# Where the constant tiles of a two-layer decoder trunk start in on-chip memory

## The chip, the core and the metric

The kernel runs on one core of one Trainium2 chip. The core has a matmul engine (TensorE, PE in the profile, with its weight loads listed apart as PEld), VectorE (DVE), ScalarE (ACT), GpSimd (POOL) and SyncE (SP), which here only issues transfers. Operands of a matmul come from the on-chip memory SBUF, 128 partitions wide; a tile takes the same range of bytes in each partition, so "a tile starts at byte 18720" means that byte of each partition. Products go to PSUM. The metric is the device time of one execution in microseconds (us); less is better.

## The reference

Two layers act on x of 512 positions by 1024 channels, in float32:

```python
for l in range(DEPTH):                      # 2
    h = rmsnorm(x, norm_mix_g[l])
    proj = einsum('bsd,de->bse', h, w_in[l])
    # split into: attention q, k, v (4 heads, two maps of 64 each), retention q, k, v, gate
    # (4 heads), short convolution b, c, x (256 each), gates of three branches (3 x 1024)
    o_da  = diff_attention(...)             # softmax map 0 minus lambda times map 1, times v
    o_ret = retention(...) * silu(r_g)
    o_sc  = sc_b * causal_dwconv(sc_c * sc_x, ...)
    y = sum over branches of sigmoid(gate + b_gate) * (o_branch @ w_branch)
    x = x + y @ w_out[l]
    h = rmsnorm(x, norm_ffn_g[l])
    g, u = split(h @ w_ffn_in[l])           # 2816 each
    x = x + (silu(causal_dwconv(g)) * u) @ w_ffn_out[l]
return x
```

## The kernel before, in words

x is held transposed, as eight tiles `x0` to `x7` of 128 channels by 512 positions (2048 bytes per partition). Every float32 product is made from operands in two parts, a rounded part (hi) and the rest (lo), by three matmuls: hi x hi, hi x lo and lo x hi (`mm3`, lines 145 to 149). Weights come as float32 tiles over SP's queue, and `split_w` (lines 130 to 140) makes their two parts with one ScalarE copy and one VectorE subtraction. The parts of x, times the gain of the norm, are made by `split_x` (lines 239 to 243) four times in the program, before the mixers and before the FFN of each layer, into tiles `xh{k}` and `xl{k}`; a pool of one buffer per name gives each new pair the place of the old one. The norm's factor itself is applied to the products.

A matmul holds a stationary operand of 128 x 128 and streams a moving operand past it. Two arrangements matter here:

- The transposed projections (`proj_T`: three parts of the short convolution for each of two halves and 24 gates, 30 tiles in a layer, product names ptsc and ptg) and the FFN's first matrix (22 tiles of g and 22 of u in a layer, pg and pu) use the weights as stationary operand and the parts of x, 512 columns, as moving one: 8 blocks of channels x 3 = 24 matmuls for each tile.
- The projections by position (`natural`, lines 301 to 330: pnrqk and pnrvg with 512 columns, pnh of each head with 384) use the parts of x as stationary operand and move the weights: 4 blocks of positions x 8 x 3 = 96 matmuls.

The other large products have no operand from x: the branches (pb, moving om, the mixers' outputs), the output projection (po0 to po7, moving y) and the FFN's second matrix (p2, moving act), all 512 columns wide.

In a layer come first pnrqk and pnrvg; then a woven stretch, in which the steps of the retention and of the heads' attention (many small VectorE and ScalarE operations between small matmuls) alternate with heads' projections, short convolution, gates and branches as filler; then gates and branch of the attention, the output projection, and the FFN in three groups of 8, 7 and 7 tiles, each with its share of the second matrix. The order on each engine is planned when the program is built, from this order in the text, by a scheduler with a model of times; waits between engines are put in by the same planner from the tiles that instructions read and write.

Tiles lie in pools, one after the other, each rounded up to a multiple of 32 bytes. In the program of before the pool of constants (`cp`) begins at byte 16512, and its tiles follow in the order in which the text first asks for them:

| Tiles | First byte | Past a multiple of 512 |
|---|---|---|
| ident, ones | 16512, 17024 | 128 |
| warm, par0, par1 | 17536, 17568, 18144 | 128, 160, 224 |
| x0 to x7 | 18720 to 33056 | 288 |
| rope_t, gtab_t | 35104, 37152 | 288 |
| mask_t, bias_t | 37280, 37792 | 416 |
| pad0, pad1 | 45984, 48064 | 416, 448 |
| state, qz0, qz1 | 50144, 53216, 57312 | 480 |
| xh0, xl0 to xh7, xl7 | 61408 to 92128 | 480 |
| rb | 94176 | 480 |

The weights' pool follows at 94208, the work tiles' pool (which holds om, y and act) at 135168 and the small tiles' pool at 219136, each a multiple of 512; the slots of the first two have sizes that are multiples of 2048 bytes.

The text that asks for the constants stands at lines 165 to 227, and for the parts of x in `split_x`:

Of the kernel before, what the change touches and what calls it, by code (L numbers as in the profile page):

```python
# [11 lines left out]
F32 = mybir.dt.float32  # L12
F32R = mybir.dt.float32r
# [24 lines left out]
SINGLE = 1  # L38
SOME = 5
# [4 lines left out]
# columns of the packed per-layer parameters  # L44
# [5 lines left out]
def trunk(ctx, tc, xT, wr, wh, wt, wda, wret, wsc, wo, wf, w2, par, lamp, relb, onehot, mask, rope, gtab, out):  # L50
# [30 lines left out]
    def weave(first, second):  # L81
        """Steps of first, each followed by about COVER us of second."""
        due = 0.0
        for _ in first:
            due += COVER
            while due > 0.0:
                cost = next(second, None)
                if cost is None:
                    break
                due -= cost  # L90
        run(second)

    def staggered(tasks):
        """Tasks side by side, a step of each at a time, each from its own start on."""
        t = 0
        while tasks:
            live = []
            for start, task in tasks:
                if start <= t and next(task, DONE) is DONE:
                    continue  # L100
                live.append((start, task))
            tasks = live
            t += 1
            yield
# [12 lines left out]
    def ordered(i):  # L117
        """The program's first loads follow one another as they are written."""
        if starting[0]:
            tc.keep_in_program_order(i)  # L120
        return i
# [23 lines left out]
    def mm3(o, a, b, start, stop):  # L145
        """o += a.T @ b in float32, from operands in two exact parts."""
        T.matmul(o, a[0], b[0], start=start, stop=False)  # L147
        T.matmul(o, a[0], b[1], start=False, stop=False)  # L148
        T.matmul(o, a[1], b[0], start=False, stop=stop)  # L149

    def split(src, hi, lo, g=None):
        """float32 src (times a column) as two float32r parts."""
        if g is None:
            A.copy(hi, src)
            V.tensor_tensor(lo, src, hi.bitcast(F32), ALU.subtract)
        else:
            A.activation(hi, src, AF.Copy, scale=g)
            V.scalar_tensor_tensor(lo, src, g, hi.bitcast(F32), ALU.mult, ALU.subtract)
        return hi, lo
# [6 lines left out]
    ident = cp.tile([P, P], F32, name="ident")  # L166
    make_identity(nc, ident)
    ones = cp.tile([P, P], F32, name="ones")
    G.memset(ones, 1.0)
    warm = cp.tile([P, 1], F32, name="warm")  # L170
    A.activation(warm, ones[:, 0:1], AF.Tanh)
    # the array's clock rises with use: bring it up while the first loads are under way
# [7 lines left out]
    x = [cp.tile([P, S], F32, name=f"x{k}") for k in range(KT)]  # L180
# [5 lines left out]
    rope_t = cp.tile([P, 2, ST, 64], F32, name="rope_t")  # L186
    gtab_t = cp.tile([P, ST, 8], F32, name="gtab_t")
    mask_t = cp.tile([P, P], F32, name="mask_t")
    bias_t = cp.tile([P, H, S], F32, name="bias_t")
# [8 lines left out]
    def biases():  # L198
        """The negated relative bias, with the causal mask, as a Toeplitz tile per head."""
        rb = cp.tile([BUCKETS + 1, H], F32, name="rb")  # L200
        V.memset(rb[BUCKETS : BUCKETS + 1], -BIG)
        G.dma_start(rb[:BUCKETS], relb)
        line = dr.tile([H, 640], F32, name="line")
        for a, b in ((0, 512), (512, 640)):
            oh = temp(f"oh{a}", b - a)[: BUCKETS + 1]
            G.dma_start(oh, onehot[:, a:b])
            ps = aux(f"psb{a}")
            T.matmul(ps[:H, : b - a], rb, oh, start=True, stop=True)
            row = temp(f"line{a}", b - a)[:H]
            V.tensor_copy(row, ps[:H, : b - a])  # L210
            G.dma_start(line[:, a:b], row)
        skew = dr.tile([H, P * 640], F32, name="skew")
        G.dma_start(skew.rearrange("h (p n) -> h p n", n=640), line.unsqueeze(1).broadcast_to([H, P, 640]))
        src = skew[:, 127 : 127 + 639 * P].rearrange("h (p n) -> p h n", n=639)
        G.dma_start(bias_t, src[:, :, :S])

    # zero columns in front of what the convolutions read
# [4 lines left out]
    # the retention's states and queries of two heads, on the diagonal blocks  # L222
    state = cp.tile([P, 2, ST - 1, P], F32R, name="state")
    G.memset(state.bitcast(F32), 0.0)
    qz = [cp.tile([P, ST, 2, P], F32R, name=f"qz{a}") for a in range(2)]
# [3 lines left out]
    def rsqrt(f, v, n, name):  # L229
        """v ** -0.5: a first guess from the exponent, and Newton's steps to float32's last bit."""  # L230
        t = sp.tile([P, n], F32, tag=f"nt{n}", name=f"nt{name}", bufs=2)
        V.tensor_scalar(t.bitcast(I32), v.bitcast(I32), 1, None, ALU.logical_shift_right)
        V.tensor_scalar(f.bitcast(I32), t.bitcast(I32), -1.0, float(0x5F3759DF), ALU.mult, ALU.add)
        for _ in range(3):
            V.scalar_tensor_tensor(t, f, -0.5, f, ALU.mult, ALU.mult)
            V.tensor_tensor(t, t, v, ALU.mult)
            V.scalar_tensor_tensor(f, t, 1.5, f, ALU.add, ALU.mult)

    def split_x(l, which, name, k):
        """x times its gain in two parts."""  # L240
        hi = cp.tile([P, S], F32R, tag=f"xh{k}", name=f"xh{k}_{name}")
        lo = cp.tile([P, S], F32R, tag=f"xl{k}", name=f"xl{k}_{name}")
        return split(x[k], hi, lo, pars[l][:, which + k : which + k + 1])

    def norm_x(name):
        """1 / rms of x by column and by row."""
# [18 lines left out]
    def project(xg, ps, w):  # L265
        """ps[e, s] = sum over d of w[d, e] x[d, s], for 128 columns of a weight."""
        for k, xk in enumerate(xg):
            sl = slice(k * P, (k + 1) * P)
            mm3(ps, (w[0][:, sl], w[1][:, sl]), xk, k == 0, k == len(xg) - 1)

    def rms_cols(sq, n, scale, name):
        """(mean square + eps) ** -0.5 over the last axis of sq [p, n, d]."""
        ms = small(n, f"ms{name}")
        V.tensor_reduce(ms, sq, AX.X, ALU.add)
        V.tensor_scalar(ms, ms, scale, EPS, ALU.mult, ALU.add)
        f = small(n, f"f{name}")
        rsqrt(f, ms, n, name)
        return f

    def transposes(src, name):  # L280
        """Four 128 x 128 blocks of src(st), side by side in a bank."""
        ps = aux(name)
        for st in range(ST):
            T.transpose(ps[:, st * P : (st + 1) * P], src(st), ident)
        return ps
# [6 lines left out]
    def layer(l):  # L292
# [8 lines left out]
        def natural(src, w, name, evacuate):  # L301
            """w columns of the input projection by position, one bank per 128 positions; in steps."""
# [70 lines left out]
        # -lambda, in every partition  # L373
# [23 lines left out]
        def head_chunk(h):  # L397
            """Head h of the attention: queries and keys by position, values in two parts."""
# [26 lines left out]
        def attention(h):  # L425
            """A head in steps: scores and softmax of a block of queries, the difference of its two
            maps, its transpose, its product with the values; neighbouring blocks overlap."""
# [3 lines left out]
            # a map's queries in two parts above each other, against keys whose first part stands twice  # L431
# [22 lines left out]
            def scores(i):  # L454
# [8 lines left out]
                for m in range(2):  # L463
                    # a map in either half of the array's rows
# [9 lines left out]
            def combine(i):  # L474
                # e0 / z0 - lambda e1 / z1, times z0
# [15 lines left out]
            def values(i):  # L491
                # against both parts of v at once, side by side
# [41 lines left out]
        kn = (wide(f"knh{L}"), wide(f"knl{L}"))  # L534

        def retention(p):
# [34 lines left out]
            def scores(b):  # L571
                # two blocks of positions, both heads
# [97 lines left out]
        def side(b, src, mats):  # L670
            """The gated sum over the short convolution (b = 2) and the retention (b = 1)."""
# [12 lines left out]
        # the retention and the heads, with what does not depend on them between their steps  # L684
# [73 lines left out]
def _consts():  # L758
    """Tables that depend on the shapes alone."""
# [18 lines left out]
    # the retention's decay between positions i and j, g ** i for queries, g ** -j / 8 for keys  # L778
# [11 lines left out]
def _layout(i):  # L790
    """The inputs as the program's tensors: tiles of weights that are contiguous by partition."""
    C = np.ascontiguousarray

    def cols(w, n):
        # [L, K*P, n*P] -> [L, n, P, K*P]
# [6 lines left out]
    def rows(w, n, width):  # L802
        # two rows of tiles beside each other
        return C(w.reshape(DEPTH, 4, 2, P, n, width).transpose(0, 4, 1, 3, 2, 5)).reshape(DEPTH, n, 4, P, 2 * width)

    def two(w):
        # two tiles of columns beside each other
# [53 lines left out]
```

## Time and profile before

| What | Value |
|---|---|
| Median of 3 runs | 1589.82 us (1586.66 to 1590.9) |
| Span of the profiled execution | 1584.9 us |
| TensorE matmuls, busy | 7286, 1577.1 us (100%) |
| VectorE busy | 980.8 us (62%) |
| ScalarE busy | 627.1 us (40%) |
| GpSimd busy | 9.1 us (1%) |
| Moved by transfers | 147.04 MB, mean 93 GB/s |
| Mean granted TensorE clock | 1.000 |

The span runs from the first to the last instruction of the profiled execution; no other time of that execution is listed, and the runs' times include what lies around it. A line of the profile names the source line (L148), the engine, the operation, the tile written and the tiles read (`out<-in`, buffer numbers and the layer's number left out), shapes, how many (x64), and times. In a table by stretches of time, each engine has its busy time and, in brackets, how many instructions ran. Matmuls are pipelined: their printed durations overlap, and a new one starts before the last has ended.

### The profile page before, as it was taken

Reading aid. Unit: us, or ns where it says so; the run is one execution under the profiler, and the core shown is the slowest. Engines: PE = TensorE matmul, PEld = TensorE weight load, DVE = VectorE, ACT = ScalarE, POOL = GpSimd, SP = SyncE. Lnnn points to the kernel's source line nnn. Section 1 sums busy time; section 2 is a strip of 40 time slices with the busy share of each in tenths; the row PEclk is TensorE's granted clock in tenths of the full one; section 3 lists DMA queues with packets and bytes.
Section 4 is the critical chain, followed back from the end, with each engine's and each line's share of the span. In section 5 each row is a group of like instructions: output and inputs, shape, how many; then the busy total and the mean of one; then the engine's idle time right before and its main releaser. Section 6 shows DMA issues by size and latency. Waiting matters only on the chain.

```text
span 1584.9 us, 18971 instructions
## 1 busy us (share of the span) xinstructions
PE 1577.1 (100%) x7286; PEld 1303.8 (82%) x7286; DVE 980.8 (62%) x1826; ACT 627.1 (40%) x1057; POOL 9.1 (1%) x21
## 2 busy tenths in 40 slices
PE   9999999999999999999999999999999999999998
PEld 7898887888888888888889988888888888888887
DVE  7488777554566456456656887765555763564562
ACT  4455664233333233233425565642333431332331
POOL 1000000000000000000000000000000000000000
PEclk9999999999999999999999999999999999999999
DMA  5322232232333332333322222322323333323323
GB/s 184 123 91 73 61 100 74 92 100 74 106 94 93 93 93 90 97 106 88 98 80 91 72 85 69 94 74 87 98 82 93 93 93 104 94 88 100 94 87 100
DMA packets 46891, 147.04 MB, mean 93 GB/s; under 512 B 6120, under 2 KB 6519, under 8 KB 46801
## 3 DMA queue, kind: packets, MB, share of 16 engines
q1 hardware_dynamic: 45216, 143.11, 30.2%
q0 software_dynamic: 1584, 2.72, 0.5%
q8 instruction: 57, 0.93, 0.3%
q14 instruction: 34, 0.27, 0.1%
HBM read 143.70 MB, written 3.42 MB: 93 GB/s over the span
## 4 chain that ended last, share of the span: by engine, by line
PE 98%; DMA 1%; DVE 0%; ACT 0%; issue 0%; SPq 0%; ACTq 0%; DVEq 0%
PE pnrvgL L147 1%; PE pnrvgL L149 1%; PE pnrvgL L148 1%; PE pnrqkL L148 1%; PE pnrqkL L149 1%; PE pnrqkL L147 1%; PE pnh3L L148 1%; PE pnh2L L149 1%; PE pnh3L L147 1%; PE pnh1L L147 1%; PE pnh2L L147 1%; PE pnh1L L148 1%; PE pnh1L L149 1%; PE pnh3L L149 1%; PE pnh2L L148 1%; PE pnh0L L147 1%
## 5 line engine op out<-in xcount | busy, mean ns | idle before, releaser
L138 ACT CAST hi_tL<-raw_tL 128x1024 fp32r<-128x1024 f32 x60 | 63.0, 1050 | 126.1 <-DMA raw_tL<-in_wt 21.8
L138 ACT CAST hi_fuL<-raw_fuL 128x1024 fp32r<-128x1024 f32 x44 | 46.3, 1052 | 156.1 <-issue 18.0
L138 ACT CAST hi_w2L<-raw_w2L 128x896 fp32r<-128x896 f32 (+1 forms) x48 | 47.1, 982 | 142.9 <-PE p200L L148 11.9
L139 DVE TENSOR_TENSOR lo_tL<-raw_tL,hi_tL 128x1024 fp32r<-128x1024 f32 x60 | 73.4, 1223 | 17.4 <-ACT hi_tL L138 17.0
L138 ACT CAST hi_fgL<-raw_fgL 128x1024 fp32r<-128x1024 f32 x44 | 46.3, 1053 | 83.8 <-issue 13.0
L139 DVE TENSOR_TENSOR lo_fuL<-raw_fuL,hi_fuL 128x1024 fp32r<-128x1024 f32 x44 | 53.9, 1225 | 27.4 <-ACT hi_fuL L138 27.4
L139 DVE TENSOR_TENSOR lo_w2L<-raw_w2L,hi_w2L 128x896 fp32r<-128x896 f32 (+1 forms) x48 | 54.4, 1133 | 3.9 <-ACT hi_w2L L138 2.3
L139 DVE TENSOR_TENSOR lo_fgL<-raw_fgL,hi_fgL 128x1024 fp32r<-128x1024 f32 x44 | 53.6, 1219 | 3.5 <-ACT hi_fgL L138 3.5
L138 ACT CAST hi_oL<-raw_oL 128x1024 fp32r<-128x1024 f32 x16 | 16.9, 1053 | 57.2 <-PE ptg7L L148 13.4
L148 PE MATMUL pnrqkL<-lo_nrqkL,xh_mL 128*128 128x512 f32 x64 | 25.6, 400 | 0.1
L149 PE MATMUL pnrvgL<-hi_nrvgL,xl_mL 128*128 128x512 f32 x64 | 25.4, 397 | 0.0
L148 PE MATMUL pnrvgL<-lo_nrvgL,xh_mL 128*128 128x512 f32 x64 | 25.4, 396 | 0.0
L149 PE MATMUL pnrqkL<-hi_nrqkL,xl_mL 128*128 128x512 f32 x64 | 25.1, 395 | 0.0
L147 PE MATMUL pnrqkL<-hi_nrqkL,xh_mL 128*128 128x512 f32 x64 | 23.7, 405 | 1.0 <-ACT hi_nrqkL L138 1.0
L147 PE MATMUL pnrvgL<-hi_nrvgL,xh_mL 128*128 128x512 f32 x64 | 24.1, 399 | 0.0
L149 PE MATMUL pnh2L<-hi_nh2L,xl_mL 128*128 128x384 f32 x64 | 22.3, 349 | 0.0
L148 PE MATMUL pnh3L<-lo_nh3L,xh_mL 128*128 128x384 f32 x64 | 22.2, 347 | 0.0
L147 PE MATMUL pnh3L<-hi_nh3L,xh_mL 128*128 128x384 f32 x64 | 22.2, 347 | 0.0
L139 DVE TENSOR_TENSOR lo_oL<-raw_oL,hi_oL 128x1024 fp32r<-128x1024 f32 x16 | 19.6, 1225 | 4.1 <-ACT hi_oL L138 4.1
L147 PE MATMUL pnh1L<-hi_nh1L,xh_mL 128*128 128x384 f32 x64 | 21.8, 341 | 0.0
L147 PE MATMUL pnh2L<-hi_nh2L,xh_mL 128*128 128x384 f32 x64 | 21.8, 340 | 0.0
L148 PE MATMUL pnh1L<-lo_nh1L,xh_mL 128*128 128x384 f32 x64 | 21.8, 340 | 0.0
(3622 smaller groups left out, 5046.7 us busy)
## 6 DMA issues: line engine op xcount, KB each, us to landing
raw_tL<-in_wt SPq DMA_DIRECT2D x60, 512.0 KB, 3.6
raw_fgL<-in_wf SPq DMA_DIRECT2D x44, 512.0 KB, 3.5
raw_fuL<-in_wf SPq DMA_DIRECT2D x44, 512.0 KB, 3.6
raw_w2L<-in_w SPq DMA_DIRECT2D x32, 448.0 KB, 3.3
raw_oL<-in_wo SPq DMA_DIRECT2D x16, 512.0 KB, 3.6
raw_w2L<-in_w SPq DMA_DIRECT2D x16, 512.0 KB, 3.5
raw_nrvgL<-in_wr SPq DMA_DIRECT2D x8, 512.0 KB, 3.6
raw_bdL<-in_wda SPq DMA_DIRECT2D x16, 256.0 KB, 2.6
```

The costliest lines, as they stand in the source:

```text
L138: A.copy(hi, raw)
L139: V.tensor_tensor(lo, raw, hi.bitcast(F32), ALU.subtract)
L147: T.matmul(o, a[0], b[0], start=start, stop=False)
L148: T.matmul(o, a[0], b[1], start=False, stop=False)
L149: T.matmul(o, a[1], b[0], start=False, stop=stop)
```

## The change

The large constant tiles are asked for at the head of the program, before any instruction, in a new order: `ident`, `ones`, a tile `fill` of 96 floats that nothing reads or writes, the eight tiles of x, eight tiles `xs` that each hold both parts of one block of x (before two tiles, `xh` and `xl`), `state`, `qz`, `rope_t`, `mask_t` and `bias_t`. After them come warm, the parameters, gtab_t, the pads and rb, in that order. `warm` has 32 columns, of which one is used as before, and `rb` 16, of which four are used. `split_x` writes into the lasting tile `xs[k]` in place of new tiles of one name. The instructions that compute, and their shapes, are the same. Comments are taken out.

```diff
+FILL = 96
...
     ident = cp.tile([P, P], F32, name="ident")
+    ones = cp.tile([P, P], F32, name="ones")
+    cp.tile([P, FILL], F32, name="fill")
+    x = [cp.tile([P, S], F32, name=f"x{k}") for k in range(KT)]
+    xs = [cp.tile([P, 2, S], F32R, name=f"xs{k}") for k in range(KT)]
+    state = cp.tile([P, 2, ST - 1, P], F32R, name="state")
+    qz = [cp.tile([P, ST, 2, P], F32R, name=f"qz{a}") for a in range(2)]
+    rope_t = cp.tile([P, 2, ST, 64], F32, name="rope_t")
+    mask_t = cp.tile([P, P], F32, name="mask_t")
+    bias_t = cp.tile([P, H, S], F32, name="bias_t")
     make_identity(nc, ident)
-    ones = cp.tile([P, P], F32, name="ones")
     G.memset(ones, 1.0)
-    warm = cp.tile([P, 1], F32, name="warm")
-    A.activation(warm, ones[:, 0:1], AF.Tanh)
+    warm = cp.tile([P, 32], F32, name="warm")
+    A.activation(warm[:, 0:1], ones[:, 0:1], AF.Tanh)
...
-    x = [cp.tile([P, S], F32, name=f"x{k}") for k in range(KT)]
...
-    rope_t = cp.tile([P, 2, ST, 64], F32, name="rope_t")
     gtab_t = cp.tile([P, ST, 8], F32, name="gtab_t")
-    mask_t = cp.tile([P, P], F32, name="mask_t")
-    bias_t = cp.tile([P, H, S], F32, name="bias_t")
...
-        rb = cp.tile([BUCKETS + 1, H], F32, name="rb")
+        rb = cp.tile([BUCKETS + 1, 16], F32, name="rb")[:, :H]
...
-    state = cp.tile([P, 2, ST - 1, P], F32R, name="state")
     G.memset(state.bitcast(F32), 0.0)
-    qz = [cp.tile([P, ST, 2, P], F32R, name=f"qz{a}") for a in range(2)]
...
     def split_x(l, which, name, k):
-        hi = cp.tile([P, S], F32R, tag=f"xh{k}", name=f"xh{k}_{name}")
-        lo = cp.tile([P, S], F32R, tag=f"xl{k}", name=f"xl{k}_{name}")
-        return split(x[k], hi, lo, pars[l][:, which + k : which + k + 1])
+        return split2(x[k], xs[k], pars[l][:, which + k : which + k + 1])
...
     def split2(src, t, g=None):
         n = src.shape[-1]
         return split(src, t[:, 0, :n], t[:, 1, :n], g)
```

## The prediction

> **What bounds the kernel now.** I read the head of the profile page first, then TensorE's waits, then the rate of matmuls in stretches that hold one kind of matmul alone.
>
> ```profile
> span 1584.9 us, 18971 instructions
> PE 1577.1 (100%) x7286; PEld 1303.8 (82%) x7286; DVE 980.8 (62%) x1826; ACT 627.1 (40%) x1057; POOL 9.1 (1%) x21
> PEclk9999999999999999999999999999999999999999
> PE 98%; DMA 1%; DVE 0%; ACT 0%; issue 0%; SPq 0%; ACTq 0%; DVEq 0%
> ...
> PE por00L L594 <- ACT PT00L L154: 1.6, 1, 1.6
> PE ps_warm L175 <- POOL ones L169: 1.1, 1, 1.1
> PE pnrqkL L147 <- ACT hi_nrqkL L138: 1.0, 1, 1.0
> ```
>
> TensorE is busy from end to end at its full granted clock, the chain of waits is 98% TensorE, and its three listed waits total 3.7 us. So the time is the number of matmuls times the distance from one start to the next. The printed durations (about 396 ns) overlap and cannot be added; the distances must be read from starts. The next rows are such stretches (PE's figure in brackets counts matmuls, two of them already under way at the left edge) and the starts at their edges.
>
> ```profile
> 385.27:428.79 43.52, 43.52 (x194) 36.05 (x193) 23.92 (x32) 15.99 (x22) 0.00 (x0) 1.00 0.31 97
> 519.70:563.24 43.54, 43.54 (x194) 36.05 (x193) 16.53 (x18) 9.09 (x10) 0.00 (x0) 1.00 0.33 97
> 563.24:641.64 78.40, 78.40 (x338) 63.12 (x336) 48.52 (x61) 27.72 (x34) 0.00 (x0) 1.00 0.30 91
> 641.64:679.75 38.11, 38.11 (x170) 31.55 (x169) 15.55 (x18) 8.45 (x10) 0.00 (x0) 1.00 0.34 99
> ...
> 385.26 0.39 PE L147 MATMUL po0L<-y0L,hi_oL 128*128 128x512 f32 x1
> 428.78 0.40 PE L147 MATMUL pg0L<-xh_fL,hi_fgL 128*128 128x512 f32 x1
> 519.69 0.39 PE L147 MATMUL p200L<-act0L,hi_w2L 128*128 128x512 f32 x1
> 563.24 0.40 PE L147 MATMUL pg8L<-xh_fL,hi_fgL 128*128 128x512 f32 x1
> 641.64 0.39 PE L147 MATMUL p210L<-act8L,hi_w2L 128*128 128x512 f32 x1
> ```
>
> The output projection (moving operand y) takes 43.52 us for 8 x 8 x 3 = 192 matmuls: 226.7 ns each. The second FFN matrix (moving act) takes 43.54 for 192 and 38.11 for 168: 226.8 ns. The first FFN matrix between them (moving xh and xl) takes 78.40 us for 14 x 24 = 336: 233.3 ns. All have the same shape, 128 x 128 stationary against 512 columns, and the same clock. At the two joins (563.24 and 641.64) the rate changes with the operand. The difference is 6.6 ns, 2.9%.
>
> What differs is where the operands start. By the addresses of the program of before, the work pools begin at byte 94208 = 184 x 512; y, act and every weight part start on multiples of 512. The parts of x start at 480 past a multiple of 512. A test from the other side: in the retention's projection x is stationary (480 past) and the weights move (on a multiple).
>
> ```profile
> 54.36 0.39 PE L148 MATMUL pnrvgL<-lo_nrvgL,xh_mL 128*128 128x512 f32 x1
> ...
> 55.76 0.39 PE L149 MATMUL pnrvgL<-hi_nrvgL,xl_mL 128*128 128x512 f32 x1
> ...
> 57.21:67.96 10.75, 10.75 (x64) 10.75 (x63) 0.00 (x0) 0.00 (x0) 1.00 0.44 131
> ```
>
> From 54.36 to 55.76 there are six steps: 233.3 ns each. So one operand off a multiple of 512, whichever, goes with 233.3. The third row is head 0's projection, 384 columns wide and x stationary: 62 matmuls in 10.75 us, 173.4 ns each.
>
> **The change part by part.** Addresses after: the constants start at 16512; ident, ones and fill add 512 + 512 + 384, which gives 17920 = 35 x 512. All eight tiles of x, xs, state, qz, rope_t, mask_t and bias_t have sizes that are multiples of 512, so all start on one. The rest (warm 128, two par 1152, gtab 128, two pads 4160, rb 64) adds 5632 = 11 x 512, and the pools then begin at 94720 = 185 x 512. No matmul, copy or load is added or dropped; the sum is starts alone.
>
> 1. Moving x parts. Per layer 30 tiles of the transposed projection and 44 of the first FFN matrix, 24 matmuls each, twice: 2 x 74 x 24 = 3552. Times 6.6 to 6.7 ns: 23.7 us.
>
> 2. Stationary x parts against 512 columns: pnrqk and pnrvg, 2 x 2 x 96 = 384, the same price: 2.6 us.
>
> 3. Stationary x parts against 384 columns, 768 matmuls. No row has this width with both operands on a multiple. One end is nothing; the other is the full 6.7 ns (5.1 us). If the cost of a good matmul goes by columns, 226.7 x 384 / 512 = 170.0, a gain of 3.4 ns. I take that, 2.6 us, since it lies between the ends.
>
> 4. Branch matmuls (om with weights, both on multiples already) follow slow ones.
>
> ```profile
> 343.53 0.40 PE L147 MATMUL ptg3L<-xh_mL,hi_tL 128*128 128x512 f32 x1
> 349.13 0.39 PE L147 MATMUL pb30L<-om0L,hi_bdL 128*128 128x512 f32 x1
> 351.88 0.40 PE L147 MATMUL ptg4L<-xh_mL,hi_tL 128*128 128x512 f32 x1
> ```
>
> Here 24 gate matmuls take 5.60 us (233.3) and 12 branch matmuls 2.75 us (229.2, not 226.7): 20 to 30 ns carried over per block. There are 48 such blocks; I take 1.0 us, between 0 and 1.4.
>
> 5. qz and state as moving operands, 84 narrower matmuls in all: between 0 and 84 x 6.7 ns = 0.6 us; I take 0.2.
>
> 6. VectorE and ScalarE on the moved tiles.
>
> ```profile
> L578 DVE TENSOR_TENSOR rd00L<-pS00L,mask_t x2: 683/686/690, 76.0 to 857.3; 128x512 f32<-128x512 f32 x2
> L252 DVE TENSOR_TENSOR ssmL<-ssmL,sq3mL x2: 683/684/685, 12.0 to 779.9; 128x512 f32<-128x512 f32 x2
> L157 ACT ACTIVATE xh_fL<-x,par x16: 715/717/720, 394.2 to 1214.2; 128x512 fp32r<-128x512 f32 x16
> ```
>
> With mask_t at 416 past a multiple a VectorE product takes 686 ns, with all operands on multiples 684, so these engines show no price for a start; and they run under TensorE. Without that cover the last x update alone would count, about 0.7 us, before and after alike. Writing both parts into one lasting tile replaces the wait for a released buffer by a wait for its last readers. The last gate of layer 0 ends before 385.26, the first FFN split starts at 394.2: 9 us late already, so the wait costs nothing; with that cover gone the price would be one split of 0.72 us. Rewritten fill, warm and rb sizes issue nothing new.
>
> The Trainium skill, SBUF — State Buffer, section Operand start alignment, says that starts on multiples of the element size are legal and that the runs behind it timed nothing. The 233.3 against 226.7 above is the timing that it lacks; it moves no term.
>
> Gross sum: 23.7 + 2.6 + 2.6 + 1.0 + 0.2 = 30.1 us. Against it stands what TensorE then waits for instead. Layer 0's 96 pnrqk matmuls follow loads and splits until the next projection starts:
>
> ```profile
> L147 PE MATMUL pnrvgL<-hi_nrvgL,xh_mL x64: 391/396/502, 31.9 to 842.2; 128*128 128x512 f32 x64
> ```
>
> In these first 32 us 96 x 6.7 ns = 0.6 us is lost. In the woven stretches TensorE alternates with the attention's VectorE and ScalarE work:
>
> ```profile
> 120.00:200.00 80.00, 80.00 (x420) 68.68 (x419) 63.37 (x178) 48.05 (x113) 0.00 (x0) 1.00 0.25 72
> 200.00:300.00 100.00, 100.00 (x482) 81.68 (x481) 72.39 (x191) 50.27 (x113) 0.00 (x0) 1.00 0.28 86
> ```
>
> VectorE, the third pair, is at 79% and 72%. The gain there is at most (1440 - 384) x 6.7 ns, for the transposed projections outside the last gates, plus 2.6 from heads: 9.7 us. VectorE has a fifth to spare against a 3% faster TensorE, so I take 1.5 us as lost, between 0 and 9.7. Net: 30.1 - 2.1 = 28.0 us.
>
> The profiled span of 1584.9 becomes 1556.9. The runs' median of 1589.82 is 4.9 above that span; with this kept, **1561.8 us**.
>
> **The rivals.**
> A. The woven stretches are paced by VectorE and their gain is lost. For it: 72 to 79% busy, and PE's longest wait (1.6 us, por00) is there. Against it: no other wait of TensorE in those stretches is listed. Remaining: FFN 2112 x 6.7 = 14.1, last gates 384 x 6.7 = 2.6, and 1.9 for layer 1's pnrqk and both pnrvg (288 matmuls): 18.6 us, so 1571.2.
>
> B. Nothing changes. The slow rate may belong to something else that goes with x's parts: where they lie (below 94208, in the constants' pool) or that a tile is re-read for long. For it: no slow operand lies in another pool, no fast one in this one. Against it: the two roles, one streaming 2048 bytes and one loading 512, both pay the same. It would also hold if a start only mattered in steps of up to 32 bytes, since every start here, 480 included, is a multiple of 32. Either way 1589.8. The Trainium skill, SBUF — State Buffer, section Specifications, gives SBUF lines of 16 bytes and a penalty per new line; by that rule both placements are equal.
>
> C. Slower: fast moving operands need multiples of 2048, not of 512. Today y, act and om start on multiples of 2048 (94208 = 46 x 2048); after, the pools lie 512 and xs 1536 past one. Then 1056 + 384 + 384 = 1824 fast matmuls drop to 233.3, 12.1 us, and x gains nothing: 1601.9. It decides as soon as moving starts at 512 past count as bad. For it: no 512-column moving operand at another fast phase is shown. Against it: weights as stationary operands start 0, 512, 1024 and 1536 past within one 226.7 stretch, and head 0's moving weights alternate between 0 and 1536 past inside the even 173.4.
>
> **How the numbers follow.** Forecast 78%, A 6%, B 10%, C 6%. The forecast's own range: gross 33.4 with nothing lost gives 1556.4; terms 3 to 5 at nothing and half of 9.7 lost gives 26.3 - 5.5 = 20.8, 1569. The runs spread over 4 us, so about 2 more on each side. To keep 8 in 10 I reach over A: 1554 to 1575. A measurement of this kernel tells about 0.3% (4.8 us) from no change. Faster by more: 78 + 6 = 84%; same: B, 10%; slower: C, 6%.
>
> **What would show it.** In the profile after, stretches of pg and pu alone should step at 226.7 ns (336 matmuls in 76.2 us instead of 78.4), pnrvg at 226.7, heads near 170, y and act unchanged at 226.7, and branch blocks without the carried 20 ns. VectorE's durations stay. Steps at 233.3 for pg mean B; steps of 233.3 for p2 mean C; new TensorE waits on VectorE or ScalarE in the woven stretches mean A. The forecast is wrong if the rate of pg stays above 230.

## The result and the profile after

The kernel with the change takes 1562.51 us, median of 4 runs (1562.17 to 1562.61), against 1589.99 us (1586.66 to 1590.90) of the kernel before beside it: a ratio of 0.9837, 95% interval 0.9823 to 0.9851. The forecast was 1561.8, in a range of 1554 to 1575. The spans of the two profiled executions, 1584.9 and 1560.0 us, are 24.9 us apart. In the later runs beside the experiments the kernel before has a median of 1586.97 us (19 runs, 1586.50 to 1590.77), 24.5 us above 1562.51. In the runs of the full kernels a run's time is 2.1 to 2.2 us above its span, so the first runs of before, with their median of 1589.99, took longer than its profiled execution, and the profiles' 24.9 is a better size of the effect than the 27.5 between the two medians.

In the two traces every engine runs the same instructions in the same order, waits on semaphores aside; only names and addresses differ. The lines numbered L148 to L150 after the change are L147 to L149 before it. First the head of the page after, and TensorE's waits.

```profile
span 1560.0 us, 18971 instructions
PE 1552.1 (99%) x7286; PEld 1302.6 (84%) x7286; DVE 980.7 (63%) x1826; ACT 627.4 (40%) x1057; POOL 9.1 (1%) x21
...
PE por00L L595 <- ACT PT00L L155: 1.8, 1, 1.8
PE ps_warm L184 <- POOL ones L178: 1.1, 1, 1.1
PE pnrqkL L148 <- ACT hi_nrqkL L139: 0.9, 2, 0.6
```

VectorE and ScalarE are as busy as before (980.8 and 627.1 us), TensorE is 25.0 us less busy with the same 7286 matmuls, and it waits for the same three things. The table by stretches after the change, for the output projection, the second FFN matrix, the first FFN matrix and the second again (span and, in PE's brackets, the matmuls, two of them already under way):

```profile
379.53:423.05 43.52, 43.52 (x194) 36.04 (x192) 23.95 (x32) 15.99 (x22) 0.00 (x0) 1.00 0.32 97
511.52:555.04 43.52, 43.52 (x194) 36.04 (x193) 16.54 (x18) 9.09 (x10) 0.00 (x0) 1.00 0.32 97
555.04:631.20 76.16, 76.16 (x338) 63.06 (x337) 48.55 (x61) 27.73 (x34) 0.00 (x0) 1.00 0.31 94
631.20:669.28 38.08, 38.08 (x170) 31.53 (x169) 15.56 (x18) 8.45 (x10) 0.00 (x0) 1.00 0.33 102
```

The 336 matmuls of the first FFN matrix take 76.16 us, 226.7 ns each, where they took 78.40. The stretches without an operand from x stay at 226.7 ns. In the retention's projection, where x is stationary, the same starts as quoted of before:

```profile
52.84 0.39 PE L150 MATMUL pnrvgL<-hi_nrvgL,xs 128*128 128x512 f32 x1
...
54.20 0.27 PE L285 MATMUL ptr0L<-ident,rr0L 128*128 128x128 f32 x1
```

Six steps in 1.36 us: 226.7 ns, where it was 233.3.

### The profile page after: what moved, and what is told of

It is laid out like the page before. It is cut to its first block, busy times and chain, and to the rows that moved or that the text cites. A ratio compares the mean times of both kernels' runs of the same rounds, so it can differ in the third digit from the quotient of the medians.

```text
span 1560.0 us, 18971 instructions
## 1 busy us (share of the span) xinstructions
PE 1552.1 (99%) x7286; PEld 1302.6 (84%) x7286; DVE 980.7 (63%) x1826; ACT 627.4 (40%) x1057; POOL 9.1 (1%) x21
## 4 chain that ended last, share of the span: by engine, by line
PE 98%; DMA 1%; DVE 0%; ACT 0%; issue 0%; SPq 0%; ACTq 0%; DVEq 0%
PE pnrvgL L150 1%; PE pnrvgL L148 1%; PE pnrvgL L149 1%; PE pnrqkL L149 1%; PE pnrqkL L150 1%; PE pnh2L L150 1%; PE pnh3L L149 1%; PE pnrqkL L148 1%; PE pnh3L L148 1%; PE pnh1L L148 1%; PE pnh2L L148 1%; PE pnh1L L149 1%; PE pnh1L L150 1%; PE pnh3L L150 1%; PE pnh2L L149 1%; PE pnh0L L148 1%
## 5 line engine op out<-in xcount | busy, mean ns | idle before, releaser
L149 PE MATMUL pnrqkL<-lo_nrqkL,xs 128*128 128x512 f32 x64 | 25.2, 394 | 0.1
L159 DVE SCALAR_TENSOR_TENSOR xs<-x,par,xs 128x512 fp32r<-128x512 f32 x32 | 23.9, 746 | 1.9 <-ACT xs L158 1.9
L150 PE MATMUL pnrvgL<-hi_nrvgL,xs 128*128 128x512 f32 x64 | 25.1, 392 | 0.0
L149 PE MATMUL pnrvgL<-lo_nrvgL,xs 128*128 128x512 f32 x64 | 25.0, 391 | 0.0
L150 PE MATMUL pnrqkL<-hi_nrqkL,xs 128*128 128x512 f32 x64 | 24.8, 390 | 0.0
L158 ACT ACTIVATE xs<-x,par 128x512 fp32r<-128x512 f32 x32 | 23.0, 717 | 3.0 <-DMA x<-in_xT 2.9
L148 PE MATMUL pnrqkL<-hi_nrqkL,xs 128*128 128x512 f32 x64 | 23.1, 397 | 0.9 <-ACT hi_nrqkL L139 0.9
L148 PE MATMUL pnrvgL<-hi_nrvgL,xs 128*128 128x512 f32 x64 | 23.8, 394 | 0.0
L150 PE MATMUL pnh2L<-hi_nh2L,xs 128*128 128x384 f32 x64 | 22.2, 348 | 0.0
L148 PE MATMUL pnh3L<-hi_nh3L,xs 128*128 128x384 f32 x64 | 22.1, 345 | 0.0
L149 PE MATMUL pnh3L<-lo_nh3L,xs 128*128 128x384 f32 x64 | 22.1, 345 | 0.0
L148 PE MATMUL pnh1L<-hi_nh1L,xs 128*128 128x384 f32 x64 | 21.8, 340 | 0.0
```

## The experiments

**Moving the block back.** Theory: the start of an operand counts. Rival: the gain comes with the new place or the merged tiles. The block of constants, from x to bias_t, is moved to 480 bytes past a multiple of 512 by 32 bytes less in front of it and 32 more behind it:

```diff
-FILL = 96
+FILL = 88
...
-    warm = cp.tile([P, 32], F32, name="warm")
+    warm = cp.tile([P, 40], F32, name="warm")
```

> The changed kernel with fill 32 bytes shorter and warm 32 bytes longer: x, xs, state, qz, rope_t, mask_t and bias_t start 480 past a multiple of 512, at otherwise the same place and with the same merged tiles; the pools behind stay on multiples. If starts count: pg, ptg and pnrvg step at 233.3 ns again and the time is that of before, 1590 us (1587 to 1592). If the gain came from the place, the order or the merged tiles (rival B's family): 1562.5, as after the change.

Measured: 1586.96 us, median of 10 runs (1586.51 to 1589.06); the ratio to the kernel before is 1.0003 (0.9994 to 1.0013). Its table by stretches, second and first FFN matrix:

```profile
519.52:563.07 43.55, 43.55 (x194) 36.04 (x193) 16.54 (x18) 9.09 (x10) 0.00 (x0) 1.00 0.32 97
563.07:641.47 78.40, 78.40 (x338) 63.12 (x337) 48.55 (x61) 27.72 (x34) 0.00 (x0) 1.00 0.30 91
```

78.40 us is the value of before to the hundredth. 32 bytes carry the whole gain; place, order and merged tiles carry nothing that can be seen. Rival B falls. (The time to compare with is the later median of before, 1586.97, and not the 1590 that was taken from its first runs.)

**The parts of x alone.** xs is asked for after bias_t, between two fillers, so that xs alone starts 480 past; x, state, qz, rope_t, mask_t, bias_t and the pools stay on multiples.

```diff
-    xs = [cp.tile([P, 2, S], F32R, name=f"xs{k}") for k in range(KT)]
...
     bias_t = cp.tile([P, H, S], F32, name="bias_t")
+    cp.tile([P, 120], F32, name="fill2")
+    xs = [cp.tile([P, 2, S], F32R, name=f"xs{k}") for k in range(KT)]
+    cp.tile([P, 8], F32, name="fill3")
```

> The changed kernel with the parts of x alone 480 past a multiple of 512; x, state, qz, rope_t, mask_t, bias_t and the pools stay on multiples. If the parts of x carry the gain, as terms 1 and 2 of the prediction say: 1588 to 1590 us. If the other tiles (VectorE's and ScalarE's reads of x, rope_t, bias_t, or qz and state) carried a share, the time lies clearly below that, towards 1575.

Measured: 1587.11 us, median of 10 runs (1586.02 to 1590.94), ratio 1.0003 (0.9993 to 1.0012). So the parts of x carry the gain, within what a measurement tells; the aligned x, rope_t, bias_t, state and qz bring nothing that can be seen.

**Everything off by the same amount.** Fill is 32 bytes shorter and nothing makes up for it, so that the pools behind move as well.

```diff
-FILL = 96
+FILL = 88
```

> The changed kernel with fill 32 bytes shorter and nothing to make up for it: the constants, the weights' pool and the work tiles' pool all start 480 past a multiple of 512, so the two operands of each large matmul are off by the same amount. If each operand's own start counts once per matmul: y, act and om slow to 233.3 as well, 1562.5 + 27 + 12 = 1602 us. If the prices of the two operands add: 5760 matmuls x 13.3 ns, about 1639. If only the distance between the two operands' starts counts (a theory that the profile of before does not exclude): nothing is lost, 1562.5.

Measured: 1562.41 us, median of 4 runs (1562.20 to 1563.60), ratio to before 0.9849 (0.9832 to 0.9865). In its table by stretches, second and first FFN matrix:

```profile
511.52:555.04 43.52, 43.52 (x194) 36.04 (x192) 16.54 (x18) 9.08 (x10) 0.00 (x0) 1.00 0.31 97
555.04:631.20 76.16, 76.16 (x338) 63.06 (x336) 48.55 (x61) 27.73 (x34) 0.00 (x0) 1.00 0.31 94
```

No part of x, no weight and no work tile of 512 columns starts on a multiple of 512 here, and both stretches are as fast as after the change. So the theory of the prediction, that an operand off a multiple of 512 pays, falls too. What is left is the distance between the starts of the two operands of a matmul: 480 against 0 before, 0 against 0 after, 480 against 480 here.

**Matmuls alone.** To measure the price by itself, rows of matmuls run with the other engines idle, over a range of starts:

```python
for r in range(REP):                        # 32
    a = m // 4 + (r % 8) * S                # S = 512; moving operand, m bytes past a multiple of 512
    b = s // 4 + (r % 8) * P                # P = 128; stationary operand, s bytes past
    T.matmul(ps[:, :n], st[:, b : b + P], mv[:, a : a + n], start=r == 0, stop=r == REP - 1)
```

> A kernel of its own that leaves out the whole computation and returns zeros: rows of 32 matmuls, each with another stationary operand of 128 x 128, for 512, 384, 256 and 128 moving columns and for different starts of the two operands. Theory of the prediction (a start on a multiple of 512 bytes is what counts): 512 columns step at 226.7 ns with both operands on a multiple, and at 233.3 ns with either one off, whether by 32, 64, 128, 256 or 480 bytes. Rival on the granularity (only a smaller line counts, say 64 bytes): 64, 128, 192, 256, 320, 384 and 448 past step at 226.7, and 32, 96 and 480 past at 233.3. Rival B (the place in the constants' pool, not the start): all steps are alike. For 384 columns the prediction took 170.0 ns with both on a multiple against 173.4 with the stationary one 480 past; the other end is 173.4 for both, that is, no price at this width.

The timeline of this kernel, one line for each row of 32 (start and length in us; the name gives columns n, moving start m and stationary start s):

```profile
15.73 7.42 PE L41 MATMUL n512m0s0x<-mvt,stt 128*128 128x512 f32 x32
30.46 7.50 PE L41 MATMUL n512m64s0x<-mvt,stt 128*128 128x512 f32 x32
52.73 7.62 PE L41 MATMUL n512m192s0x<-mvt,stt 128*128 128x512 f32 x32
60.19 7.44 PE L41 MATMUL n512m256s0x<-mvt,stt 128*128 128x512 f32 x32
89.70 7.62 PE L41 MATMUL n512m480s0x<-mvt,stt 128*128 128x512 f32 x32
104.62 7.63 PE L41 MATMUL n512m0s64x<-mvt,stt 128*128 128x512 f32 x32
119.51 7.42 PE L41 MATMUL n512m0s256x<-mvt,stt 128*128 128x512 f32 x32
134.21 7.63 PE L41 MATMUL n512m0s480x<-mvt,stt 128*128 128x512 f32 x32
141.68 7.44 PE L41 MATMUL n512m480s480x<-mvt,stt 128*128 128x512 f32 x32
148.96 7.51 PE L41 MATMUL n512m32s480x<-mvt,stt 128*128 128x512 f32 x32
...
170.88 5.73 PE L41 MATMUL n384m0s0x<-mvt,stt 128*128 128x384 f32 x32
187.59 5.82 PE L41 MATMUL n384m0s480x<-mvt,stt 128*128 128x384 f32 x32
```

A row's step is its length less one matmul (0.39 us at 512 columns, 0.34 at 384), over 31. From the starts, leaving out the first eight of each row:

| Moving minus stationary start, bytes, past a multiple of 256 | Cases (moving/stationary) | Step at 512 columns, ns |
|---|---|---|
| 0 | 0/0, 256/0, 0/256, 256/256, 480/480, 64/64 | 226.7 (64/64: 227.1) |
| 32 | 32/0, 0/480 | 233.3 |
| 64 | 64/0, 320/0, 32/480 | 228.9 to 229.0 |
| 96 | 96/0 | 233.5 |
| 128 | 128/0, 384/0, 0/128, 0/384 | 232.1 to 233.5 |
| 192 | 192/0, 448/0, 0/64 | 233.2 to 233.3 |
| 224 | 480/0, 0/32 | 233.3 |

The case 64/0 is not slow in the way that 0/64 is, and 32/480 agrees with 64/0: the sign counts, and what counts is the difference, with a period of 256 bytes. Neither of the two theories on record of which starts are good holds. The two steps 226.7 and 233.3 of the full kernel are there with no other engine at work, so the price needs none.

At 384 columns 0/0 and 480/0 step at 173.4 ns and 0/480 at 176.8. No distance gives the 170.0 that the prediction assumed. At 256 columns the steps are 119.7 (0/0), 118.2 (480/0) and 116.5 (0/480), at 128 columns 111.7 for all three: at these widths a distance of 0 is no better than the others.

**Two distances in the full kernel.** If the distance counts, a block 256 past must be as good as one on a multiple of 512, and a block 64 past must cost different amounts with x moving and with x stationary. The block was moved as above, with fill of 160 or 112 floats, and warm of 96 or 16 to bring the pools back onto a multiple.

> The changed kernel with the block of constants 256 bytes past a multiple of 512, all else as after. If the distance counts with a period of 256 bytes: 1562.5 us, as after the change. If multiples of 512 are needed, as the change has it: 1587.

Measured: 1564.08 us, median of 4 runs (1562.76 to 1564.46), ratio to before 0.9853 (0.9837 to 0.9870), an interval that overlaps that of the change. Its span is 1.6 us longer than after the change. Layer 0's pnrqk, which waits for loads, takes 25.87 us in it against 24.59 after and 25.81 before; in the sums of matmul steps this projection holds 1.3 of the 1.6 us, while layer 1's pnrqk and both pnrvg, with the same starts, take what they take after the change (22.0 and 44.4 us). So most of the 1.6 us is no price of the distance.

```profile
6.16:32.03 25.87, 24.52 (x108) 19.10 (x109) 21.31 (x45) 14.44 (x21) 0.00 (x0) 1.00 0.67 212
```

> The changed kernel with the block of constants 64 bytes past a multiple of 512, all else as after. By the distances measured with matmuls alone: the 3552 matmuls with moving x parts are 64 past their weights (228.9 ns, 2.2 over), the 384 with stationary x parts 64 the other way (233.3, 6.6 over): 1562.5 + 7.9 + 2.5 = 1573 us. By a theory in which any start off a multiple of 256 or 512 costs the full price: 1587. By one in which multiples of 64 are good: 1562.5.

Measured: 1573.96 us, median of 4 runs (1573.64 to 1574.28), ratio 0.9917 (0.9902 to 0.9932), against 1573 worked out from the matmuls alone. The second and first FFN matrix:

```profile
516.21:559.78 43.57, 43.57 (x194) 36.03 (x193) 16.54 (x18) 9.10 (x10) 0.00 (x0) 1.00 0.32 97
559.78:636.70 76.92, 76.92 (x338) 63.10 (x337) 48.54 (x61) 27.70 (x34) 0.00 (x0) 1.00 0.31 93
```

76.92 us for 336 is 228.9 ns, the step of 64/0 in the row of matmuls alone. The other role, x stationary, in layer 0's pnrvg:

```profile
53.91 0.39 PE L150 MATMUL pnrvgL<-hi_nrvgL,xs 128*128 128x512 f32 x1
...
55.31 0.27 PE L285 MATMUL ptr0L<-ident,rr0L 128*128 128x128 f32 x1
```

Six steps in 1.40 us are 233.3 ns, the step of 0/64. So distances measured with matmuls alone carry over to the full kernel.

**Which pair, and is another distance better?** A finer scan, and rows in which both starts go round 0, 32 and 128, so that the moving operand agrees with the stationary one of its own matmul, of the next or of the one before.

> A kernel of its own that leaves out the whole computation and returns zeros: rows of 48 matmuls of 512 columns. First a finer scan of the distance d between the starts of the moving and the stationary operand. If the price belongs to the distance with a period of 256 bytes, all steps lie between 226.7 ns (d = 0) and about 233.5, with 64 at 229; none is below 226.7 unless some distance is better than 0. Then three rows in which both operands' starts go round 0, 32 and 128 past, so that each matmul's moving operand agrees with the stationary operand of the same matmul (own), of the one after (next) or of the one before (prev). If the moving stream collides with the weight load of the next matmul, which runs beside it: next steps at 226.7, own and prev near 233. If it is the matmul's own pair of operands that counts: own at 226.7, next and prev near 233. At last the same stationary bytes again and again, with d = 0 and 32: if what counts is starts, 226.7 and 233.3 as with changing ones; if a repeated operand is not read again, both 226.7 or less.

Timeline, rows of 48 (a step is the length less 0.39, over 47):

```profile
19.52 11.04 PE L37 MATMUL d0x<-mvt,stt 128*128 128x512 f32 x48
30.40 11.48 PE L37 MATMUL d4x<-mvt,stt 128*128 128x512 f32 x48
86.42 11.20 PE L37 MATMUL d48x<-mvt,stt 128*128 128x512 f32 x48
141.96 11.04 PE L37 MATMUL d112x<-mvt,stt 128*128 128x512 f32 x48
208.92 11.05 PE L37 MATMUL d240x<-mvt,stt 128*128 128x512 f32 x48
219.81 11.32 PE L37 MATMUL ownx<-mvt,stt 128*128 128x512 f32 x48
230.97 11.15 PE L37 MATMUL nextx<-mvt,stt 128*128 128x512 f32 x48
241.96 11.31 PE L37 MATMUL prevx<-mvt,stt 128*128 128x512 f32 x48
275.26 11.09 PE L37 MATMUL samed0x<-mvt,stt 128*128 128x512 f32 x48
286.19 11.37 PE L37 MATMUL samed32x<-mvt,stt 128*128 128x512 f32 x48
```

From the starts: distances of 0, 112 and 240 step at 226.7 ns, 48 at 230.0, 64 at 228.9; the other thirteen lie between 231.1 (80) and 235.3 (4). None is below 226.7, so nothing is to be had beyond the change by another distance. Own and prev step at 232.4, next at 228.9, and the same again when own and next were repeated. With these three starts, a moving stream that agrees with the stationary operand of the next matmul gets about two thirds of the gain, not the whole of it that was expected, and one that agrees with its own or the previous one hardly any. With the same stationary bytes every time the steps are 226.8 and 233.3, and the trace lists 48 weight loads for the 48 matmuls: a repeated operand is loaded again.

**Does a shorter weight load cost less?** The last kernel varied the number of stationary columns.

> A kernel of its own that leaves out the whole computation and returns zeros: rows of 48 matmuls with 512, 448 or 384 moving columns and stationary operands of 128, 96, 64 or 32 columns, at distances d of 0, 32 and 144 bytes (and more for 384). If the price is a collision with the weight load that runs beside the stream, a load of half the columns reads half as long and the price at d = 32 shrinks with it, from 6.6 ns to about 3.3 at 64 columns and 1.7 at 32. If it is a price per matmul for the starts as such, it stays 6.6 ns at every number of stationary columns. For 384 moving columns the first look gave 173.4 ns at d = 0 and 224 and 176.8 at d = 32: by the collision theory the price there goes up and down with d and never below 173.4; by the prediction's column rule a good distance would step at 170.0.

Timeline (w is the number of stationary columns):

```profile
19.01 11.04 PE L36 MATMUL n512w128d0x<-mvt,stt 128*128 128x512 f32 x48
29.89 11.37 PE L36 MATMUL n512w128d32x<-mvt,stt 128*128 128x512 f32 x48
52.30 11.21 PE L36 MATMUL n512w96d0x<-mvt,stt 128*96 128x512 f32 x48
74.54 11.05 PE L36 MATMUL n512w96d144x<-mvt,stt 128*96 128x512 f32 x48
85.42 11.21 PE L36 MATMUL n512w64d0x<-mvt,stt 128*64 128x512 f32 x48
140.90 11.43 PE L36 MATMUL n512w32d144x<-mvt,stt 128*32 128x512 f32 x48
```

| Stationary columns | d = 0 | d = 32 | d = 144 |
|---|---|---|---|
| 128 | 226.7 | 233.3 | 233.3 |
| 96 | 230.0 | 233.4 | 226.7 |
| 64 | 229.9 | 230.8 | 230.0 |
| 32 | 231.7 | 233.0 | 235.5 |

(Steps in ns from the starts, 512 moving columns.) Both expectations fail. The difference between d = 32 and d = 0 does shrink, 6.6, 3.4, 0.9 and 1.3 ns from 128 to 32 columns, but mostly because d = 0 becomes slower (226.7 to 231.7): with 64 and 32 columns none of the three distances is back at 226.7. It is no fixed price of a pair of starts either: with 96 columns 144 is the good distance and 0 is not. At 448 moving columns the steps are 202.7 (0) and 206.7 (32 and 144). At 384 they lie between 173.3 (distances 0, 32, 64 and 160) and 176.7 (96), never below.

At 384 columns the distance alone does not settle the step. 32/0 steps at 173.3 here and 0/480, the same distance modulo 256, at 176.8 above; and in the kernel before, heads with the same pair of starts step at 173.4 in one stretch (57.21 to 67.96, shown in the prediction) and at 176.7 in another (146.47 to 150.71, shown below). The rule of the distance is shown for 512 columns.

## Why the prediction was right, and where it was not

The direction, the place and the price per matmul were right: 6.6 ns for each matmul of 512 columns with a part of x. The reason given for it was wrong. "One operand off a multiple of 512" fitted every row of the trace before, because there every good pair lay on multiples; the experiment with everything 480 past takes it away. The distance between the operands explains the 512-column stretches of all the full kernels. The change works because it brings x and the weights to the same phase (start modulo 256), not because it brings them to multiples of 512. Rival B is excluded by the block moved back. Rival C is excluded by the profile after: pools 512 and xs 1536 past a multiple of 2048 run at 226.7.

By stretches. Between the starts of the two profiles, the first FFN matrix gains 13.8 us in both layers (predicted 14.1), the last gates with their branches 3.0, the woven stretches 5.1 and the projections ahead of them 2.8: 24.7 of the 24.9 us. Before and after, the last gates of layer 0 and the two woven stretches:

```profile
318.49:385.27 66.78, 66.78 (x290) 54.10 (x289) 35.27 (x47) 22.35 (x31) 0.00 (x0) 1.00 0.31 95
...
55.99:318.49 262.50, 260.93 (x1352) 223.54 (x1350) 192.77 (x507) 139.07 (x307) 1.73 (x2) 1.00 0.29 88
842.92:1102.97 260.05, 260.05 (x1347) 222.92 (x1346) 192.74 (x504) 138.68 (x306) 0.00 (x0) 1.00 0.26 80
```

```profile
314.25:379.53 65.28, 65.28 (x290) 54.05 (x288) 35.29 (x47) 22.23 (x31) 0.00 (x0) 1.00 0.31 97
...
54.21:314.25 260.04, 258.27 (x1352) 223.33 (x1350) 192.66 (x507) 139.18 (x307) 1.59 (x2) 1.00 0.28 89
829.16:1086.57 257.41, 257.41 (x1347) 222.73 (x1345) 192.72 (x504) 139.00 (x306) 0.00 (x0) 1.00 0.26 80
```

- Terms 1 and 2, matmuls of 512 columns: 26.3 us gross. The sums of matmul steps by product fall by 21.1 us for term 1 (23.7 gross) and 2.8 for term 2 (2.6). That term 2 comes so near is in part luck: 1.2 of the 2.8 come from layer 0's pnrqk, whose sum lies between 22.7 and 24.7 us in the seven full kernels and does not follow the distance; layer 1's gives 0.5, the two pnrvg 1.0.
- Term 3, heads at 384 columns: this step failed. Predicted 2.6 us by scaling a good matmul with its columns; the sums give 0.2 (137.2 to 137.0 us). Most heads stepped at 173.4 ns before and do so after; the other stretches, of 15 to 24 matmuls at 176.4 to 177.0, became 173.3, and part of that is lost again because some stretches now begin with steps of up to 185 ns. The prediction had read one stretch of head 0, a good one. Before and after, one of the others:

```profile
146.47:150.71 4.24, 4.24 (x26) 4.24 (x26) 4.11 (x8) 4.13 (x8) 0.00 (x0) 1.00 0.28 113
```

```profile
144.35:148.51 4.16, 4.16 (x26) 4.16 (x25) 4.06 (x7) 4.05 (x8) 0.00 (x0) 1.00 0.30 109
```

- Term 4, the branches' carried time: predicted 1.0, by the sums 0.8 (89.4 to 88.6). The last gates alone gain 1.50 us a layer: 192 gate matmuls at 6.67 ns are 1.28, eight branch blocks the other 0.22, 27 ns each, in the range read from the trace.
- Term 5, qz and state: predicted 0.2, within the noise of the woven stretch (the sums of the score matmuls go up by 0.3).
- Term 6 was right: VectorE's product with mask_t takes 688 ns where it took 686, and the merged tiles brought no wait.
- The loss in the woven stretches was named and under-sized: of 1056 x 6.67 = 7.0 us for the transposed projections and some 0.8 for 32 branch blocks, 5.1 arrived, so about 2.7 us were lost where 1.5 was taken. The reason given for it was wrong too. The prediction expected VectorE to hold TensorE up, but TensorE's idle time in the two stretches above is 1.6 us before and 1.8 after, all in layer 0. What falls short is its own steps: of the gates and short convolutions there, the 488 matmuls that stand eight or more behind the first one in a row for the same product fall from 233.3 to 227.1 ns, the 470 that stand one to seven behind it only from 232.9 to 229.8. Just after a change of product the good distance brings about half. Rival A, which loses all of it to VectorE, did not come. The 0.6 us of loss at the start did not come: layer 0's pnrqk gains 1.2 us. But in the block 256 past it gains nothing, so this stretch varies by more than its term.

The net gain of 28.0 us was therefore 3.1 too high against the profiles' 24.9. The time still came within 0.7 us, since a second term was off the other way: the prediction kept the 4.9 us by which the first runs of before exceeded its profiled span, and after the change that margin is 2.5 us (1562.51 against 1560.0). The two errors nearly cancel, and that is luck: the 4.9 held what the first runs of before took beyond its profiled execution, which has nothing to do with the change.

## What to carry to other kernels

When TensorE sets the end, read the distance between starts of matmuls in stretches of one kind and compare stretches of the same shape: a difference of 3% that follows the operand is worth a look at the list of addresses. What is to be made equal is the phase of the two operands of a matmul, modulo 256 bytes for 128 x 128 by 512 in this kernel; at 384 columns and fewer the runs here show little or no gain. And an agreement between good rows (here: all on multiples of 512) is not yet the rule: a kernel in which both operands are off by the same amount tells the two apart.

## What the runs showed of the hardware that was not expected

The step of a matmul depends on where its two operands lie relative to each other. The Trainium skill, SBUF — State Buffer, section Who interferes with whom, gives TensorE two independent read ports, one for the moving operand and one for weight loads, and says that only the port pair of VectorE and GpSimd causes contention. The rows of matmuls alone differ: with no other engine at work the step is 226.7 ns or 233.3 by nothing but the distance of the two operands, and in the one set of starts that was tried the next matmul's stationary operand matters most (228.9 against 232.4). The measurement decides.

What the mechanism is stays open. That the pair with the next matmul counts points to the weight load that runs beside a stream, but with loads of a half or a quarter of the columns no step measured is back at 226.7 (229.9 to 235.5), the good distances change with the number of stationary columns, and at 384 moving columns the same distance of 32 steps at 173.3 or at 176.8. A matmul that follows a change of operands goes through some five or more uneven steps before it settles (the 20 to 30 ns of a branch block, the half gain of the woven stretches). That, and the two steps of the heads with the same starts, looks like two sequences that fall into step. No run here tells more than that.
